# Tokens' operands 64 bytes past multiples of 128 where they stream, at multiples of 128 where weights stream

## The chip, the cores and the metric

The kernel runs on one core of one Trainium2 chip. The metric is the device time of one execution in microseconds (us), the median of several runs. A core has five engines that run side by side: TensorE (PE, matrix products, with its weight loads shown apart as PEld), VectorE (DVE), ScalarE (ACT), GpSimd (POOL) and SyncE (SP), whose queue issues the loads of the weights. Data lie in a memory of 128 partitions; an offset in this text is always in bytes along one partition.

## The reference

What is computed is a stack of transformer-like layers over 256 tokens of width 1024, in float32: a first block of two layers (a recurrent and windowed-attention mixer, a dense feed-forward, a gated delta-rule mixer, a layer of eight experts of which each token uses two), and a second block of two layers, each a feed-forward, a convolution and gating mixer, and a feed-forward.

```python
def swiglu(h, w_gate, w_up, w_down):
    return (jax.nn.silu(h @ w_gate) * (h @ w_up)) @ w_down

# first block, layer 0 and layer 1 (j = 0)
h = h + even_mixer(rms_norm(h, ln_mix[0]), ...)
h = h + swiglu(rms_norm(h, ln_ffn[0]), ...)            # 1024 -> 2816 -> 1024
h = h + gated_deltanet(rms_norm(h, ln_mix[1]), ...)
h = h + moe_swiglu(rms_norm(h, ln_ffn[1]), ...)        # 8 experts, 1024 -> 3584 -> 1024, top 2
# second block, twice
x = x + 0.5 * swiglu_ffn(rms_norm_2(x, ffn1_norm), ...)  # 1024 -> 2816 -> 1024
x = x + mixer(rms_norm_2(x, mix_norm), ...)              # convolution, spatial gate, short convolution
x = x + 0.5 * swiglu_ffn(rms_norm_2(x, ffn2_norm), ...)
```

The result is the last sum after a final norm. All weights, some 590 MB, are read once.

## The kernel before

The residual `X` stays on the chip as [channel, token]: 8 tiles of 128 channels x 256 tokens. Every part reads the norm's operands and adds its product to `X`.

**Single-pass products.** A float32 operand is split into two float32r parts, high and low, and a product is made in three passes: high x high, high x low, low x high. Weights are split by `weights_` (lines 224 to 243): a load of 1 MB into `raw`, then `hi` by ACT (line 231) and `lo` by DVE (line 232), in rings of 4 raw, 5 hi and 5 lo tiles. The tokens' parts are `xh` and `xl`, written by `gain_split` (lines 318 to 324) when a part closes (`acc_close_`, line 308).

**Two ways to multiply.** `mm3` (lines 241 to 250) keeps the weights still, a 128 x 128 block of hi or lo, and streams 256 columns of tokens. `gemm_a` uses it with xh and xl for gates, ups and the mixers' inputs (output tile `bank`); `acc_add` uses it for the products into the residual (output `side`), with the parts `hh` and `hl` of a feed-forward, `yh` and `yl` of the first mixer, or the two halves of `o2` of the delta-rule mixer. `mm3t` (lines 252 to 256) keeps 128 tokens still and streams 512 (in places 256) columns of weights: for q, k and v of the first mixer, the gates of the delta-rule mixer, one product of the later mixers, and all of the experts. A few products of the mixers use whole float32 operands (`mm3` with two operands, line 245) and are not touched.

**Experts.** They run in four pairs. `prep` gathers a pair's tokens, at most 128 for each expert: the even pairs (0 and 2) into tiles of their own, `xeh` and `xel`, the odd pairs (1 and 3) into `xh` and `xl`. An expert takes seven chunks of 512 hidden columns: gate and up are 2 x 8 blocks x 3 passes = 48 matmuls a chunk (336 an expert), the gated product `mh` comes from ACT and DVE (lines 1175, 1176), four transposes, the split into `mhh` and `mhl`, and down, 4 x 2 x 3 = 24 matmuls a chunk (168 an expert). The order of the queues is made by a scheduler from priorities; the change touches none of them.

**Where the operands lie.** Pools are laid one behind the other. The weights' rings start at a multiple of 128 bytes. The tile `p0` has 600 columns, 2400 bytes, which is 96 beyond a multiple of 128, and the tiles behind it inherit that. In the program as built, the bytes beyond a multiple of 128 are:

| tile | before | after | its part in a product |
|---|---|---|---|
| hi, lo | 0 | 0 | still in `mm3`, streams in `mm3t` |
| xh, xl in the mixers and feed-forwards | 96 | 64 | streams in `mm3`; still in the mixers' `mm3t` |
| xh, xl in the experts (odd pairs) | 96 | 0 | still |
| xeh, xel (even pairs) | 0 | 0 | still |
| mhh, mhl | 96 | 0 | still |
| hh, hl of the feed-forwards | 0 | 64 | streams |
| yh, yl of the first mixer | 0 | 64 | streams |
| o2, both halves | 64 | 64 | streams |

The column "after" follows from the diff: 64 for slices that start at element 16 of a tile at a multiple of 128, 0 for `mhh`, whose tiles start at 96 and whose slices start 32 bytes on.

Of the kernel before, what the change touches and what calls it, by code (L numbers as in the profile page):

```python
# [7 lines left out]
F32 = mybir.dt.float32  # L8
F32R = mybir.dt.float32r
I32 = mybir.dt.int32  # L10
AF = mybir.ActivationFunctionType
# [15 lines left out]
W32 = (1, 1, 1, 0)  # L27


# ---------------------------------------------------------------- host layout  # L30
class Pack:
    """Columns of one [128, n] array; name -> column range."""
# [14 lines left out]
def cols(v):  # L47
    """[n*128] -> [128, n], channel c*128+p at [p, c]."""
    return np.asarray(v).reshape(-1, 128).T


def rows(v):
    """[n] on every partition."""
    v = np.asarray(v).reshape(1, -1)
    return np.broadcast_to(v, (128, v.shape[1]))
# [91 lines left out]
# ---------------------------------------------------------------- kernel  # L147
class Builder:
    def __init__(self, ctx, tc, dram, at, out):
# [11 lines left out]
        self.turn, self.half = 0, False  # L161
        self.p0 = self.cp.tile([128, dram["p0"].shape[1]], F32, name="p0")
        self.X = self.cp.tile([128, KD, T], F32, name="X")
        xv = dram["x"].rearrange("(k p) t -> p k t", p=128)
        with tc.high_priority(offset=100000):
            nc.sync.dma_start(self.p0, dram["p0"])
            for k in range(0, KD, 2):
# [6 lines left out]
        self.xh = self.cp.tile([128, KD, T], F32R, name="xh")  # L174
        self.xl = self.cp.tile([128, KD, T], F32R, name="xl")
        # the router takes the gains of its norm
# [3 lines left out]
                                ALU.mult)  # L180

# [10 lines left out]
    def bank(self):  # L192
        """for products with weights"""
        return self.ps.tile([128, 512], F32, name="bank", bufs=4)

    def side(self):
        """for everything else"""
        self.turn = 0 if self.half else 1 - self.turn
        return self.ps.tile([128, 512], F32, name=f"side{self.turn}", bufs=2)

    def other(self):
        """while half is set, what side() leaves"""
        return self.ps.tile([128, 512], F32, name="side1", bufs=2)

    # ---- weights: one raw load, split into two float32r parts
# [7 lines left out]
    def weights(self, ap, kt, n, raw=None, whole=False):  # L213
        """k -> (hi, lo) of rows k*128.. of ap, or those rows themselves"""
# [26 lines left out]
    def mm3(self, out, *ops, start, stop):  # L241
        """three passes over (w hi, w lo, x hi, x lo), or the engine's own float32 product of (w, x)"""
# [15 lines left out]
    # ---- [d, token] products: out rows = columns of W  # L258
    def gemm_a(self, W, c0, n, evac, x32=None):
        """for blocks of up to 512 columns: banks of [128, 2, 256] to evac(bank, first col tile)."""  # L260
# [19 lines left out]
    # ---- products into the residual: 4 banks hold [d, token]  # L280
# [3 lines left out]
    def acc_add(self, W, r0, kt, h, first, last, new=None):  # L284
        """acc += W[r0:r0+kt*128, :]^T h, h whole or in two parts; two k-tiles to a load."""
# [14 lines left out]
    def acc_close(self, scale, gain):  # L300
        """X += scale * acc, with the next norm's operands."""
# [6 lines left out]
    def acc_close_(self, scale, gain):  # L308
        nc = self.nc
        for j in range(4):  # L310
# [15 lines left out]
    # ---- 1/sqrt of small tiles  # L326
# [18 lines left out]
    def rms_(self):  # L345
        """rstd of X over d: [token, 2] and, along the free axis, [128, token]."""
# [45 lines left out]
    # ---- dense feed-forward  # L392
    def ffn(self, wg, wu, wd, nff, scale, gain):
        nc, tc = self.nc, self.tc
        with tc.tile_pool(name="ffn", bufs=2) as pl:
            prev = None
            v2 = lambda t: t.rearrange("p (a t) -> p a t", a=2)
            for f0 in range(0, nff, 512):
                w = min(512, nff - f0)
                hh = pl.tile([128, 4, T], F32R, name="hh")  # L400
                hl = pl.tile([128, 4, T], F32R, name="hl")
# [25 lines left out]
    # ---- recurrent + windowed attention mixer  # L427
    def mixer0(self, gain):
# [3 lines left out]
        with tc.tile_pool(name="mx0", bufs=1) as pl, tc.tile_pool(name="mx0w", bufs=2) as wl:  # L432
            yh = pl.tile([128, 4, T], F32R, name="yh")
            yl = pl.tile([128, 4, T], F32R, name="yl")
            # rope tables with the gains in them
# [9 lines left out]
            # softplus(-lam)  # L445
# [5 lines left out]
            # recurrent input and gates  # L451
# [13 lines left out]
            # q, k, v in [token, column]  # L465
# [28 lines left out]
            # a = exp(-8 r softplus); with t = tanh(4 r softplus) sqrt(1 - a^2) = (1 + a) sqrt(t)  # L494
# [70 lines left out]
            # attention of one block of 128 queries, the even or the odd heads at a time  # L565
# [64 lines left out]
    def softplus(self, pl, out, x, sign, n, tag):  # L630
        """log(1 + exp(sign*x)) = max(sign*x, 0) + 2 atanh(e/(2+e)), e = exp(-|x|)."""
# [18 lines left out]
    # ---- gated delta rule  # L650
    def gdn(self, gain):
# [9 lines left out]
        with tc.tile_pool(name="gd", bufs=1) as pl, tc.tile_pool(name="gdw", bufs=3) as wk, \  # L661
                tc.tile_pool(name="gdd", bufs=1, space=bass.MemoryType.DRAM) as dp:
            # decay and write strength: the last 128 columns of w_in hold them in rows 112..127
# [4 lines left out]
            with first():  # L668
# [23 lines left out]
                # columns: sums around the middle of each block; what follows in block 0  # L692
# [6 lines left out]
                # decays of [j, i]: block 0, block 0 to 1, block 1  # L699
# [18 lines left out]
            # projections with the causal convolution  # L718
# [17 lines left out]
            def sums(src):  # L736
                """|src|^2 + eps of two heads: [token, (m, head)]"""
# [24 lines left out]
            # strictly lower coefficients, transposed: [j, i] of block 0, block 1, block 0 to 1  # L762
# [24 lines left out]
            def evac_q_(bk, c, n):  # L787
                conv(bk, c, qT[:, c:c + 2])
                # eps * 128 * (|q|^2 + eps), what the norm of the unscaled rows adds
# [25 lines left out]
            # y: the coefficients' inverse applied to the values; then outputs [token, d], normed per head  # L815
# [42 lines left out]
            # gates [token, d], then the product as [d, token]  # L858
# [28 lines left out]
    def unit_blocks(self, pl, wk, dp, L):  # L887
        """(I + L)^-1 of the 16 x 16 blocks on the diagonal, one to a partition, and the transposes."""
# [3 lines left out]
        d1 = dp.tile([16, 8, 16, 16], F32, name="d1")         # block and head, b, j, i  # L892
        d2 = dp.tile([2, 16, 8, 16, 16], F32, name="d2")
        lt = pl.tile([128, 272], F32, name="lt")              # [j][i]
        z = pl.tile([128, 272], F32, name="z16")              # [r][c]
# [10 lines left out]
        # 4 x 4 by substitution  # L906
# [9 lines left out]
        # then twice the size: the lower left block is -(right one) (coefficients) (left one)  # L916
# [525 lines left out]
```

## Time and profile before

| | us |
|---|---|
| median of 3 runs | 2518.41 |
| lowest and highest run | 2515.88, 2519.7 |
| span of the profiled execution | 2515.8 |

The stages, by the time at which each closes into the residual: first mixer to 104 us, its feed-forward to 298, delta-rule mixer to 489, experts to 1545, then feed-forward to 1735, mixer to 1835, feed-forward to 2025, feed-forward to 2217, mixer to 2314, feed-forward to the end. The profile counts an engine as busy while an instruction of it is in the works. Matmuls overlap, so a group's mean duration (about 283 ns at 256 columns) is longer than the distance from one start to the next. Where the time order is shown, each row has the start, the duration, the engine, the line and the tiles as out<-in; the stationary and the streamed operand stand behind the arrow.

### The profile page before, as it was taken

How to read it: one execution, taken by the hardware profiler on the slowest of the kernel's cores; microseconds unless marked ns; L12 is line 12 of the kernel's file. 1: busy time of each engine (PE TensorE's matmuls, PEld its weight loads, DVE VectorE, ACT ScalarE, POOL GpSimd, SP SyncE). 2: the span in 40 equal slices, each digit the busy share in tenths (PEclk: the TensorE clock that was granted, in tenths of full speed). 3: DMA queues.
4: the chain of work that ended last, by engine and by line, in shares of the span. 5: the costliest groups of instructions: out<-in, count | busy, mean ns of one | idle time of the engine just before them, and what ended most of it. 6: DMA issues, size and time to landing. Idle time of an engine off the chain costs nothing.

```text
span 2515.8 us, 38995 instructions
## 1 busy us (share of the span) xinstructions
PE 2461.9 (98%) x15762; PEld 2211.6 (88%) x15762; DVE 1885.2 (75%) x2550; ACT 1422.3 (57%) x1761; POOL 19.0 (1%) x41
## 2 busy tenths in 40 slices
PE   7999999999999999999999999999999999999999
PEld 7899999887787778777777778999899999998998
DVE  7765696788988888888898888556865575587554
ACT  6544572477776777777767776445144444443443
POOL 0000000000000000000000000000000000000000
PEclk9999999999999999999999999999999999999999
DMA  6455542589898999999999997554465555545552
GB/s 220 148 176 190 171 140 81 183 293 342 309 334 302 349 343 333 330 351 347 344 324 348 339 353 275 194 170 149 144 207 190 184 168 191 175 131 183 185 184 84
DMA packets 269084, 595.22 MB, mean 237 GB/s; under 512 B 15776, under 2 KB 43808, under 8 KB 268896
## 3 DMA queue, kind: packets, MB, share of 16 engines
q1 hardware_dynamic: 268240, 590.52, 68.3%
q8 instruction: 125, 2.05, 0.3%
q0 software_dynamic: 368, 1.88, 0.2%
q14 instruction: 63, 0.52, 0.1%
q10 hardware_dynamic: 288, 0.26, 0.0%
HBM read 591.18 MB, written 1.44 MB: 236 GB/s over the span
## 4 chain that ended last, share of the span: by engine, by line
PE 57%; DVE 8%; ACT 2%; DMA 2%; issue 1%; DVEq 0%; ACTq 0%
PE bank L249 7%; PE bank L250 7%; PE bank L248 7%; PE bank L255 6%; PE bank L256 6%; PE bank L254 6%; PE side L249 3%; PE side L248 3%; PE side L250 3%; DVE av L1287 3%; DVE lo L232 3%; PE side L254 2%; PE side L255 2%; PE side L256 2%; ACT hi L231 2%
## 5 line engine op out<-in xcount | busy, mean ns | idle before, releaser
L232 DVE TENSOR_TENSOR lo<-raw,hi 128x1024 fp32r<-128x1024 f32 (+1 forms) x1077 | 1270.4, 1217 | 397.8 <-ACT hi L231 390.6
L231 ACT CAST hi<-raw 128x1024 fp32r<-128x1024 f32 (+1 forms) x1077 | 1081.0, 1046 | 573.4 <-PE bank L249 249.9
L248 PE MATMUL bank<-xh,hi 128*128 128x256 f32 x2152 | 608.6, 283 | 15.4 <-ACT hi L231 11.0
L249 PE MATMUL bank<-xl,hi 128*128 128x256 f32 x2152 | 610.9, 284 | 0.3
L250 PE MATMUL bank<-xh,lo 128*128 128x256 f32 x2152 | 609.5, 284 | 0.0
L248 PEld LDWEIGHTS bank<-xh,hi 128*128 128x128 f32 x2152 | 408.8, 190 | 17.0 <-ACT hi L231 11.0
L249 PEld LDWEIGHTS bank<-xl,hi 128*128 128x128 f32 x2152 | 406.5, 189 | 1.2 <-DVE xl L323 0.9
L250 PEld LDWEIGHTS bank<-xh,lo 128*128 128x128 f32 x2152 | 405.8, 189 | 0.3
L249 PE MATMUL side<-hl,hi 128*128 128x256 f32 x880 | 249.2, 283 | 0.0
L250 PE MATMUL side<-hh,lo 128*128 128x256 f32 x880 | 249.1, 283 | 0.0
L248 PE MATMUL side<-hh,hi 128*128 128x256 f32 x880 | 249.0, 283 | 0.0
L255 PE MATMUL bank<-lo,xh 128*128 128x512 f32 (+1 forms) x544 | 215.2, 396 | 6.3 <-DVE lo L232 6.3
L254 PE MATMUL bank<-hi,xh 128*128 128x512 f32 (+1 forms) x544 | 211.3, 388 | 4.0 <-PEq L1074 4.0
L256 PE MATMUL bank<-hi,xl 128*128 128x512 f32 (+1 forms) x544 | 210.7, 387 | 0.0
L255 PE MATMUL bank<-lo,xeh 128*128 128x512 f32 x448 | 178.1, 397 | 4.7 <-DVE lo L232 4.2
L255 PE MATMUL side<-lo,mhh 128*128 128x512 f32 x448 | 181.4, 405 | 0.5 <-DVE lo L232 0.2
L254 PE MATMUL bank<-hi,xeh 128*128 128x512 f32 x448 | 175.8, 392 | 1.1 <-ACT hi L231 1.1
L256 PE MATMUL side<-hi,mhl 128*128 128x512 f32 x448 | 176.9, 397 | 0.0
L256 PE MATMUL bank<-hi,xel 128*128 128x512 f32 x448 | 175.1, 391 | 0.0
L250 PEld LDWEIGHTS side<-hh,lo 128*128 128x128 f32 x880 | 168.9, 192 | 0.0
L248 PEld LDWEIGHTS side<-hh,hi 128*128 128x128 f32 x880 | 168.8, 192 | 0.0
L249 PEld LDWEIGHTS side<-hl,hi 128*128 128x128 f32 x880 | 168.8, 192 | 0.0
(421 smaller groups left out, 2894.1 us busy)
## 6 DMA issues: line engine op xcount, KB each, us to landing
raw<-in_o_moe_w_down_dram SPq DMA_DIRECT2D x112, 1024.0 KB, 6.8
raw<-in_o_moe_w_up_dram SPq DMA_DIRECT2D x111, 1024.0 KB, 7.0
raw<-in_o_moe_w_gate_dram SPq DMA_DIRECT2D x109, 1024.0 KB, 7.0
raw<-in_ffn_w_gate_dram SPq DMA_DIRECT2D x44, 1024.0 KB, 5.2
raw<-in_ffn_w_up_dram SPq DMA_DIRECT2D x44, 1024.0 KB, 5.1
raw<-in_ffn_w_down_dram SPq DMA_DIRECT2D x44, 1024.0 KB, 5.1
raw<-in_o_w_in_dram SPq DMA_DIRECT2D x16, 1024.0 KB, 5.4
raw<-in_w_in_dram SPq DMA_DIRECT2D x20, 768.0 KB, 4.5
```

Of the source, the lines that this page charges most:

```text
L231: nc.scalar.copy(hi[:, :w], src)
L232: nc.vector.tensor_tensor(lo[:, :w], src, hi[:, :w], ALU.subtract)
L248: nc.tensor.matmul(out, wh, xh, start=start, stop=False, skip_group_check=True)
L249: nc.tensor.matmul(out, wh, xl, start=False, stop=False, skip_group_check=True)
L250: nc.tensor.matmul(out, wl, xh, start=False, stop=stop, skip_group_check=True)
L254: nc.tensor.matmul(out, xh, wh, start=start, stop=False, skip_group_check=True)
L255: nc.tensor.matmul(out, xh, wl, start=False, stop=False, skip_group_check=True)
L256: nc.tensor.matmul(out, xl, wh, start=False, stop=stop, skip_group_check=True)
L1287: nc.vector.scalar_tensor_tensor(av[:, c], ca[:, c, j:j + T], caw[:, c, j:j + 1], av[:, c], ALU.mult, ALU.add)
```

## The change

The tiles of xh and xl grow by 32 columns, are made first in their pool (so they start at a multiple of 128), and `place` sets which slice of them is in use: element 0 for the step "ffn1", the experts, and element 16 (64 bytes) for every other step. `acc_close_` calls it before it writes the next step's operands. hh, hl, yh and yl come from `stream`, a tile with 32 columns more of which the slice from element 16 is used. mhh and mhl get 32 columns more and a slice from element 8, 32 bytes on, which puts them at multiples of 128. Nothing else of the program differs, apart from comments.

```diff
+OFF = 16
@@ Builder.__init__
+        self.xs = [self.cp.tile([128, KD * T + 32], F32R, name=n) for n in ("xh", "xl")]
+        self.place("mix0")
         self.p0 = self.cp.tile([128, dram["p0"].shape[1]], F32, name="p0")
...
-        self.xh = self.cp.tile([128, KD, T], F32R, name="xh")
-        self.xl = self.cp.tile([128, KD, T], F32R, name="xl")
...
+    def place(self, step):
+        o = 0 if step == "ffn1" else OFF
+        self.xh, self.xl = (t[:, o:o + KD * T].rearrange("p (k t) -> p k t", k=KD) for t in self.xs)
+
+    def stream(self, pool, k, name):
+        t = pool.tile([128, k * T + 32], F32R, name=name)
+        return t[:, OFF:OFF + k * T].rearrange("p (k t) -> p k t", k=k)
@@ acc_close_
         nc = self.nc
+        if gain is not None:
+            self.place(gain)
@@ ffn
-                hh = pl.tile([128, 4, T], F32R, name="hh")
-                hl = pl.tile([128, 4, T], F32R, name="hl")
+                hh, hl = self.stream(pl, 4, "hh"), self.stream(pl, 4, "hl")
@@ mixer0
-            yh = pl.tile([128, 4, T], F32R, name="yh")
-            yl = pl.tile([128, 4, T], F32R, name="yl")
+            yh, yl = self.stream(pl, 4, "yh"), self.stream(pl, 4, "yl")
@@ moe_pass
-                hh, hl = wk.tile([128, 4, 128], F32R, name="mhh"), wk.tile([128, 4, 128], F32R, name="mhl")
+                hh, hl = (wk.tile([128, 544], F32R, name=n)[:, 8:520].rearrange("p (a t) -> p a t", a=4)
+                          for n in ("mhh", "mhl"))
```

## Rows read from the trace of the kernel before

**Rows 1.** The page's head: span, and busy time and share of each engine.

```profile
span 2515.8 us, 38995 instructions
PE 2461.9 (98%) x15762; PEld 2211.6 (88%) x15762; DVE 1885.2 (75%) x2550; ACT 1422.3 (57%) x1761; POOL 19.0 (1%) x41
```

**Rows 2.** Stages: length, busy us by engine, PE clock, DMA share, GB/s.

```profile
107.00:310.00 203.00, 202.83 (x1683) 201.94 (x1683) 128.02 (x164) 95.72 (x113) 3.98 (x5) 1.00 0.55 183
310.00:500.00 190.00, 183.58 (x1386) 171.92 (x1384) 148.26 (x365) 94.77 (x172) 4.34 (x5) 0.99 0.40 129
1020.00:1280.00 260.00, 255.47 (x1151) 203.84 (x1150) 224.95 (x219) 187.63 (x209) 0.00 (x0) 1.00 0.97 343
1740.00:1810.00 70.00, 68.07 (x413) 61.62 (x413) 64.82 (x164) 16.86 (x29) 0.00 (x0) 1.00 0.45 143
```

**Rows 3.** The chain of work, 1740 to 1810 us, shares by line.

```profile
by line: DVE av L1287 53.4%; DVE lo L232 9.3%; issue 5.1%; DVE t L1235 3.7%; DVE cc L1306 3.4%; PE side L245 1.9%; ACT hi L231 1.5%; DVE cb L1235 1.3%; DVE cc L1235 1.3%; DVE y L1314 1.3%; PE bank L250 1.2%; PE bank L248 1.2%; PE bank L249 
```

**Rows 4.** PE in time order, 256 columns: start us, us, line, tiles, count.

```profile
199.92 0.28 PE L249 MATMUL bank<-xl,hi 128*128 128x256 f32 x1
...
206.04 0.28 PE L249 MATMUL bank<-xl,hi 128*128 128x256 f32 x1
...
221.88 0.28 PE L249 MATMUL side<-hl,hi 128*128 128x256 f32 x1
...
228.00 0.28 PE L249 MATMUL side<-hl,hi 128*128 128x256 f32 x1
...
463.05 0.28 PE L249 MATMUL side<-o,hi 128*128 128x256 f32 x1
...
465.99 0.28 PE L250 MATMUL side<-o,lo 128*128 128x256 f32 x1
...
469.38 0.28 PE L249 MATMUL side<-o,hi 128*128 128x256 f32 x1
...
480.94 0.28 PE L249 MATMUL side<-o,hi 128*128 128x256 f32 x1
```

**Rows 5.** PE in time order, experts, 512 columns, weights streaming.

```profile
1096.12 0.39 PE L255 MATMUL bank<-lo,xeh 128*128 128x512 f32 x1
...
1101.11 0.39 PE L256 MATMUL bank<-hi,xel 128*128 128x512 f32 x1
...
1300.26 0.40 PE L254 MATMUL bank<-hi,xh 128*128 128x512 f32 x1
...
1305.89 0.40 PE L254 MATMUL bank<-hi,xh 128*128 128x512 f32 x1
...
1309.37 0.40 PE L255 MATMUL side<-lo,mhh 128*128 128x512 f32 x1
...
1311.47 0.40 PE L256 MATMUL side<-hi,mhl 128*128 128x512 f32 x1
```

**Rows 6.** Groups by line, whole span: count, busy us, mean ns, idle.

```profile
L248 PE MATMUL bank<-xh,hi 128*128 128x256 f32 x2152 | 608.6, 283 | 15.4 <-ACT hi L231 11.0 <-ACT xh L322 2.2 <-ACT lg L491 2.1
...
L248 PE MATMUL side<-hh,hi 128*128 128x256 f32 x880 | 249.0, 283 | 0.0
```

**Rows 7.** DVE in time order: line 1176 in experts 4 and 6.

```profile
1039.43 0.74 DVE L1176 SCALAR_TENSOR_TENSOR mh<-bank,gs,mh 128x512 f32<-128x512 f32 x1
...
1140.89 0.75 DVE L1176 SCALAR_TENSOR_TENSOR mh<-bank,gs,mh 128x512 f32<-128x512 f32 x1
...
1297.33 0.74 DVE L1176 SCALAR_TENSOR_TENSOR mh<-bank,gs,mh 128x512 f32<-128x512 f32 x1
...
1399.83 0.74 DVE L1176 SCALAR_TENSOR_TENSOR mh<-bank,gs,mh 128x512 f32<-128x512 f32 x1
```

**Rows 8.** Stages, two stretches of experts 4 and 6.

```profile
1039.40:1140.90 101.50, 99.73 (x435) 78.29 (x434) 86.42 (x82) 72.77 (x80) 0.00 (x0) 1.00 0.98 353
1297.30:1399.80 102.50, 100.90 (x435) 78.53 (x434) 86.56 (x81) 72.33 (x79) 0.00 (x0) 1.00 0.98 348
```

**Rows 9.** Load queue waits, 500 to 1545 us: total us, times, longest.

```profile
SPq L209 <- DVE lo L232: 889.4, 329, 12.3
```

## The prediction

> **What bounds the kernel now.** I read the page's head first: PE is busy 98% of a span of 2515.8 us, DVE 75%, ACT 57% [rows 1]. An average hides stages, so the second view is the busy time by stage [rows 2]. In the first dense feed-forward (107 to 310 us) PE works 202.83 of 203 us, while DVE stands at 128 and the DMA engines near half: PE alone sets the time there, and the four later ones are the same code. In the delta-rule mixer (310 to 500) PE has 183.58 of 190. In the first of the two later mixers (1740 to 1810) PE is busy 68.07 of 70 and DVE 64.82, and the chain of work decides: 53.4% of it is DVE's long convolution [rows 3]. In the experts (1020 to 1280) PE is busy 255.47 of 260, but the DMA engines are at 0.97 as well, so two resources are near their end together.
>
> A busy PE says nothing of its pace, because matmuls overlap in the trace. The pace is the distance from one start to the next. The change alters nothing but where operands begin, and the kernel before already holds several cases of this, side by side, so the trace can price it. Which tile lies where is in the table ahead of this.
>
> 256 columns, weights stationary at 0: tokens streamed from 96 (xh, xl) take 51 steps in 199.92 to 206.04, 120.0 ns each; tokens streamed from 0 (hh, hl) take 51 steps in 221.88 to 228.00, 120.0 ns; tokens streamed from 64 (the parts of o2, product of the delta-rule mixer) take 102 steps in 469.38 to 480.94, 113.3 ns [rows 4]. Same lines, same shape, and in all three the chip granted PE its upper clock level of 2.4 GHz (1.00, or 0.99 over the stage, in [rows 2]). One exception has to be kept: o2's first k-tile, 463.05 to 465.99, runs 25 steps at 117.6 ns at the same offset.
>
> 512 columns, weights streaming from 0: tokens stationary at 0 (xeh, xel) take 22 steps in 1096.12 to 1101.11, 226.8 ns; at 96 (xh, xl used for odd pairs) 24 steps in 1300.26 to 1305.89, 234.6 ns; at 96 (mhh, mhl) 9 steps in 1309.37 to 1311.47, 233.3 ns [rows 5].
>
> **Part by part.** No instruction is added, removed or moved, and no DMA. Moving xh by 64 bytes makes a k-slice overlap two old slices, so a write of xh could wait for readers of both; all those readers are products that PE finishes before the products into the residual, whose last one the write waits for anyway. Nothing is queued behind a new wait. The extra bytes in SBUF cost no time.
>
> *Dense feed-forward, five times.* Gate and up are 2 x 22 x 8 = 352 blocks, down 176, three passes each: 528 x 3 = 1584 matmuls, 7920 in all; of the 2152 rows a pass for xh [rows 6] these are 1760, and all 880 of hh. Both streams go to 64. The saving is 120.0 - 113.3 = 6.7 ns each: 7920 x 6.7 = 53.1 us. Nothing hides it, since PE has no idle time in the stage, and what is late next is far off: at 113.3 ns a feed-forward needs 1584 x 0.1133 = 179 us where DVE works 128 and DMA about 0.55 x 203 = 112 us [rows 2]. The low end of the gain is o2's first k-tile: 120.0 - 117.6 = 2.4 ns, 19 us. I take 113.3, since seven of o2's eight k-tiles run so, through stalls and transposes in between.
>
> *Delta-rule mixer and small mixers.* The same offset for 2152 - 1760 = 392 blocks of xh and mixer0's 32 of yh, three passes: 1272 x 6.7 = 8.5 us. The later mixers hold 384 of these matmuls; part stands beside the convolution on DVE [rows 3], so I count half of their 2.6 us, and of the other 5.9 all but 0.7, for stretches that wait on DVE's chains: 6.5 us, ends 3 and 8.5. Here tokens also stand still at 64 while weights stream (q, k, v, the delta-rule gates, the values of the later mixers): 144 matmuls of 512 columns and 144 of 256. No row has that combination. Its neighbours are 226.8 ns at 0 and 234.6 at 96, so 7.8 ns either way, 288 x 7.8 = 2.2 us gain or loss; I take 0, no change from today, which lies between these ends.
>
> *Experts.* Gate and up of the odd pairs go from 96 to 0: 4 experts x 336 = 1344 matmuls x (234.6 - 226.8) = 10.5 us. Down of all experts too: 8 x 168 = 1344 x (233.3 - 226.8) = 8.7 us. Together 19.2 us of PE time. How much of it arrives is read from two like stretches, from an expert's first product of gate and up on DVE (mh, line 1176) to its seventh. Expert 4 has its tokens at 0, expert 6 at 96, otherwise the same work: 288 gate and up matmuls, so 288 x 7.8 = 2.2 us apart in pace. They take 101.5 us (1039.43 to 1140.89) and 102.5 (1297.33 to 1399.83), 1.0 apart [rows 7]. So 0.45 of the pace arrived. The reason stands beside it: DMA at 0.98 in both stretches, 353 and 348 GB/s [rows 8]. The queue of loads waits 889.4 us for raw buffers that DVE frees [rows 9], so a faster PE does ask for loads sooner, but the engines have 2% left. I take 19.2 x 0.45 = 8.7 us, ends 0 and 19.2. The Trainium skill ("HBM Reference", Specifications) says that a core streaming alone gets about 425 GB/s; by it the experts, at about 350, would have room, the whole 19.2 would arrive and the sum would be 10.5 us better. The 0.98 of the rows speaks against it, and they decide.
>
> Sum: 53.1 + 6.5 + 8.7 = 68.3 us. The profiled execution's span is 2515.8 us, against a median of 2518.41 of the runs, which reach from 2515.88 to 2519.7; the 2.6 us between lie around the span or in the runs' own spread, and the change touches neither. 2518.4 - 68.3 = 2450.1 us.
>
> **Rivals.**
> *Two paces at 64.* Whether a stream at 64 settles at 113.3 or 117.6 ns may depend on how it was entered, and long unbroken feed-forward streams keep what they start with. If half of them hold 117.6, the feed-forwards give 0.5 x 53.1 + 0.5 x 19 = 36 us, the mixers 4, the experts 8.7: 49 us, 2469.6 us. All of them at 117.6, 19 + 2 + 8.7: 2489 us. For: 25 steps in [rows 4]. Against: the next k-tile is entered by the same four transposes and does settle.
> *The offset is not the cause.* o2's product could be faster for another reason, as its stage. Then only the experts' gain stands, and with DMA at its end perhaps not even that: 2510 to 2518 us. A page has this as a rule: the Trainium skill ("TensorE: Matmul & The Clock Gate", Wait — 56ns, not 53.3ns?) gives the distance of warm matmuls as columns over 2.4 GHz plus 2.5 ns, with no word of addresses; by it 256 columns take 109 ns wherever they lie, and the time stays at 2518. The trace disagrees: 113.3 and 120.0 ns for the same shape, both above 109. Against the rival as such: xeh and xh differ by 7.8 ns in the same code of the same stage [rows 5].
> *Slower: the two parts collide.* The parts now lie 8320 bytes apart (xh, xl) and 4224 (hh, hl) instead of 8192 and 4096. If the second pass starting in the other half of a 256-byte line costs what an unlucky start costs now, 6.7 ns more than today instead of less, on every pass, 9192 x 6.7 = 62 us come on top, less 8.7: about 2571 us. It decides from the point at which more than half of the passes pay, as then the mean exceeds 120.0. Against it: parts 8192 and 4096 apart both run at 120.0 [rows 4]; no row has an odd multiple of 128.
> *Experts fully bound by DMA*: 2518.4 - 59.6 = 2458.8 us; *not bound*: 2439.6 us. Both lie within the forecast's own range.
>
> **How the numbers follow.** Forecast with its experts' ends 0.85; two paces 0.08; offset not the cause 0.04; slower 0.03. The time is the forecast's, 2450. The forecast alone reaches from 2518.4 - 53.1 - 8.5 - 2.2 - 19.2 = 2435 to 2518.4 - 53.1 - 3 + 2.2 - 0 = 2464.5. The range takes in also the half-way case of two paces: 2435 to 2472. About 0.2% (5 us) is what a measurement can tell from no change. Faster by more: forecast, two paces and a part of the third, 0.94; within 0.2%: 0.03; slower 0.03.
>
> **What would show it.** In the profile after, xh, xl, hh and hl steps of 113.3 ns in every feed-forward, so that a stage of 190 us loses 10 to 11; expert 6's stretch at about 101 us with DMA at 0.98 or more, gate and up at 226.8 ns and down too; mixers nearly as long as before. Steps of 117.6 ns in whole feed-forwards would bear out the first rival, 120.0 the second, and steps of hi with xl alone above 120 the third. If the experts lose 19 us, DMA was not at its end and my factor of 0.45 is wrong.

## The result, and the profile after

The changed kernel takes 2488.28 us (median of 4 runs, 2487.47 to 2490.13) against 2517.93 us before: a ratio of 0.9883, 95% interval 0.9871 to 0.9895. The forecast was 2450 us with a range from 2435 to 2472. The sign is right, the gain is 30 us instead of 68, and the time lies outside the range.

The head of the page after: span, then busy time, share and count of each engine. It answers [rows 1].

```profile
span 2485.8 us, 38995 instructions
PE 2430.1 (98%) x15762; PEld 2187.8 (88%) x15762; DVE 1884.9 (76%) x2550; ACT 1422.0 (57%) x1761; POOL 19.9 (1%) x41
```

Same counts, nearly the same shares: PE's own time fell by 31.8 us, the span by 30.0. PE is still what the kernel waits for. Busy time by stage after (stretch, length, busy us and count of PE, PEld, DVE, ACT and POOL, PE clock, DMA share, GB/s), a feed-forward and the experts, answers [rows 2]:

```profile
107.00:295.00 188.00, 187.58 (x1597) 186.98 (x1596) 118.00 (x139) 88.35 (x103) 3.61 (x2) 1.00 0.57 188
1020.00:1280.00 260.00, 255.28 (x1160) 204.92 (x1159) 225.77 (x220) 187.77 (x208) 0.00 (x0) 1.00 0.97 344
```

Nothing new ends last: PE fills the feed-forward at the upper clock level (1.00, 2.4 GHz), and the experts still have PE and DMA near their ends. So the question is PE's pace. PE in time order after, 256 columns (start us, us, line, tiles, count), first and last row of four unbroken stretches: the high and low parts of xh, hh in its first buffer, hh in its second, and o2.

```profile
204.81 0.28 PE L259 MATMUL bank<-xh,hi 128*128 128x256 f32 x1
...
217.68 0.28 PE L261 MATMUL bank<-xh,lo 128*128 128x256 f32 x1
...
218.15 0.28 PE L259 MATMUL side<-hh,hi 128*128 128x256 f32 x1
...
225.93 0.28 PE L259 MATMUL side<-hh,hi 128*128 128x256 f32 x1
...
252.07 0.28 PE L259 MATMUL side<-hh,hi 128*128 128x256 f32 x1
...
259.91 0.28 PE L259 MATMUL side<-hh,hi 128*128 128x256 f32 x1
...
466.74 0.28 PE L259 MATMUL side<-o,hi 128*128 128x256 f32 x1
...
478.40 0.28 PE L259 MATMUL side<-o,hi 128*128 128x256 f32 x1
```

110 steps of xh at 117.0 ns, 66 of hh at 117.9, 69 of hh in its other buffer at 113.6, and 99 of o2 at 117.8. Two things stand out. The two buffers of hh, written and read by the same lines, differ by 4.3 ns. And o2, whose offset the change left alone, slowed from the 113.3 ns of [rows 4] to 117.8.

Offsets beyond a multiple of 128, as the prediction counted them, can't tell the buffers of hh apart: both are 64. Taken beyond a multiple of 256 they can. In the program as built, hi and lo lie at 128 beyond a multiple of 256, before and after. Below, the distance of an operand is its own place minus that of the weights, within 256 bytes (so +64 and -64 differ, and -128 is the farthest).

| operand | distance before | distance after | mean step before | after |
|---|---|---|---|---|
| xh, xl (streams) | +96, +96 | +64, -64 | 120.0 ns | 117.4 ns |
| hh, hl, first buffer | 0, 0 | +64, +64 | 119.9 | 117.8 |
| hh, hl, second buffer | 0, 0 | -64, -64 | 119.9 | 114.3 |
| o2, both halves | -64 | -64 | 114.1 | 117.5 |
| xh, xl still, experts | +96, +96 | 0, -128 | 234.2 | 231.4 |
| mhh still, one buffer pair | +96 | -128 | 234.2 | 232.7 |
| mhh still, the other pair | +96 | 0 | 234.2 | 227.9 |

The means are over all undisturbed steps of the span, with each matmul of the trace joined to its operands' addresses in the program. A tile of 8320 bytes is an odd multiple of 128, so xl lands on the other side of the weights than xh; tiles of 4224 bytes do the same to successive buffers. The experts in time order after, 512 columns, odd pair, answer [rows 5]:

```profile
1291.65 0.40 PE L266 MATMUL bank<-lo,xh 128*128 128x512 f32 x1
...
1296.73 0.40 PE L267 MATMUL bank<-hi,xl 128*128 128x512 f32 x1
```

22 steps at 230.9 ns, between the 234.6 and 226.8 of [rows 5].

By stage (from one stage's last addition to X to the next one's) the five feed-forwards went from 966.3 to 944.6 us, the experts from 1055.5 to 1048.9, and the mixers from 494.0 to 492.3: 21.7, 6.6 and 1.6 us before rounding, which is the whole difference of the spans, 30.0 us.

### The profile page after: what moved, and what is told of

The parts are those of the page before. It is cut to its first block, busy times and chain, and to the rows that moved or that the text cites. A ratio compares the mean times of both kernels' runs of the same rounds, so it can differ in the third digit from the quotient of the medians.

```text
span 2485.8 us, 38995 instructions
## 1 busy us (share of the span) xinstructions
PE 2430.1 (98%) x15762; PEld 2187.8 (88%) x15762; DVE 1884.9 (76%) x2550; ACT 1422.0 (57%) x1761; POOL 19.9 (1%) x41
## 4 chain that ended last, share of the span: by engine, by line
PE 56%; DVE 8%; ACT 2%; issue 1%; DMA 1%; DVEq 0%; ACTq 0%
PE bank L266 7%; PE bank L261 6%; PE bank L260 6%; PE bank L259 6%; PE bank L267 6%; PE bank L265 6%; PE side L260 3%; PE side L261 3%; PE side L259 3%; DVE av L1299 3%; DVE lo L243 3%; PE side L265 3%; PE side L266 2%; PE side L267 2%; ACT hi L242 2%
```

## The experiments

Theory A: what counts is the distance between the two operands within 256 bytes, and both token parts have to lie alike; the change misses 113.3 ns because its parts don't. Rivals: the absolute place counts; the pace depends on how the stream was entered; the DMA engines eat the experts' gain. In the table "us" is the median of a kernel's runs, while the stage lengths (us) come from the one execution that was traced; for e5 that is the quickest of its four, for e4 the slowest.

| kernel | distance of the streams | us | ratio to before (95%) | feed-forwards | experts |
|---|---|---|---|---|---|
| before | +96; 0 | 2517.9 | | 193.9 189.7 190.8 191.4 200.6 | 1055.5 |
| the change | +64/-64; +64 or -64 | 2488.3 | 0.9883 (0.9871 to 0.9895) | 189.7 185.4 186.4 187.0 196.0 | 1048.9 |
| e1 | -64 | 2454.8 | 0.9760 (0.9743 to 0.9776) | 184.3 180.2 180.0 182.0 190.9 | 1043.6 |
| e2 | +64 | 2475.7 | 0.9824 (0.9806 to 0.9842) | 190.8 186.4 186.4 181.9 190.9 | 1043.9 |
| e3 | many | 2493.5 | one run | 191.2 186.0 186.6 190.2 199.5 | 1046.8 |
| e4 | as the change | 2492.9 | 0.9901 (0.9885 to 0.9918) | 189.7 185.4 186.4 187.3 196.3 | 1055.4 |
| e5 | -64, weights moved | 2475.9 | 0.9842 (0.9823 to 0.9861) | 184.4 180.2 181.0 188.3 191.0 | 1048.4 |
| e6 | -64 high, +64 low | 2489.9 | 0.9890 (0.9873 to 0.9906) | 190.8 186.4 186.4 188.3 197.4 | 1043.4 |
| e7 | -64 | 2493.4 | one run | 190.8 186.4 187.4 181.9 197.3 | 1056.1 |
| e8 | -64 | 2447.0 | one run | 184.4 192.5 186.4 188.3 197.3 | 1004.1 |
| e9 | +64, with entries | 2503.0 | one run | 193.0 188.2 188.7 190.5 199.6 | 1045.0 |
| e10 | -64, with entries | 2468.9 | one run | 186.8 182.2 183.2 184.4 193.3 | 1043.7 |
| e11 | -64, with entries | 2483.7 | one run | 186.8 182.2 183.5 184.4 193.7 | 1056.8 |

**Both parts on one side.** e1 puts every streamed part 64 bytes short of the weights and every still part of the experts on the weights' own class; the tiles grow by 64 columns, so successive tiles stay alike.

```diff
-OFF = 16
+OFF = 48
...
-        self.xs = [self.cp.tile([128, KD * T + 32], F32R, name=n) for n in ("xh", "xl")]
+        self.xs = [self.cp.tile([128, KD * T + 64], F32R, name=n) for n in ("xh", "xl")]
...
-        t = pool.tile([128, k * T + 32], F32R, name=name)
+        t = pool.tile([128, k * T + 64], F32R, name=name)
...
-                hh, hl = (wk.tile([128, 544], F32R, name=n)[:, 8:520].rearrange("p (a t) -> p a t", a=4)
+                hh, hl = (wk.tile([128, 576], F32R, name=n)[:, 40:552].rearrange("p (a t) -> p a t", a=4)
```

> The tiles grow by 64 columns instead of 32, so both parts and both buffers lie alike modulo 256: every streamed token operand 64 bytes below the weights' class (192 above it modulo 256), every stationary one of the experts in the weights' class. Theory A (the place modulo 256 relative to the weights sets the pace): all streams at 113.3 to 114.5 ns. From 117.4 for xh that is 6456 x 3.5 = 23 us, from 117.8 for the first buffer of hh 1440 x 4 = 6 us, the experts' gate and up of odd pairs and half of down 3 to 4 ns faster each, some 5 us of which arrive; about 34 us less than the changed kernel, 2454 us. Theory B (only modulo 128 counts, and whether a stream settles at 113.3 or 117.6 is decided by how it was entered): the mixture stays, 2485 to 2491 us.

Measured 2454.8 us (2453.8, 2455.7, 2461.8, 2453.9). PE in time order of e1, in a late feed-forward and in an odd pair of the experts:

```profile
1899.93 0.28 PE L259 MATMUL bank<-xh,hi 128*128 128x256 f32 x1
...
1909.90 0.28 PE L260 MATMUL side<-hl,hi 128*128 128x256 f32 x1
...
1282.83 0.39 PE L266 MATMUL bank<-lo,xh 128*128 128x512 f32 x1
...
1285.77 0.39 PE L267 MATMUL bank<-hi,xl 128*128 128x512 f32 x1
```

88 steps at 113.3 ns, across both kinds of product, and 13 at 226.2 in the experts. The feed-forwards gain 48.9 us on before, the experts 11.9, the mixers 3.3: together 64, near the 68.3 of the prediction's sum. This is the version that beats both kernels.

**The other side.** e2 is e1 with `OFF = 16`: both parts 64 bytes past the weights.

> As the run before, but the streams lie 64 bytes above the weights' class modulo 256 instead of 64 below; the same place modulo 128. Theory A: all streams of xh and hh at 117.8 ns and none at 113.3, the experts as in the run before: 6456 x 0.4 + 1200 x 3.4 = 6.5 us more and some 5 us less than the changed kernel, about 2490 us. Theory B: hh and xh keep stretches at 113.3 ns, as today about 0.4 of hh; 2480 to 2488 us.

Measured 2475.7 us (2475.2, 2476.1, 2467.8, 2476.1). PE in time order of e2, in two neighbouring feed-forwards:

```profile
1899.89 0.28 PE L261 MATMUL side<-hh,lo 128*128 128x256 f32 x1
...
1909.90 0.28 PE L259 MATMUL bank<-xh,hi 128*128 128x256 f32 x1
...
2079.91 0.28 PE L261 MATMUL bank<-xh,lo 128*128 128x256 f32 x1
...
2090.00 0.28 PE L260 MATMUL side<-hl,hi 128*128 128x256 f32 x1
```

85 steps at 117.8 ns and 89 at 113.4: the same code at the same distance. DVE in time order of e2, the last addition to X of three stages, shows that it holds for the whole stage:

```profile
1815.91 0.69 DVE L325 SCALAR_TENSOR_TENSOR X<-side,X 128x512 f32<-128x512 f32 x1
...
2002.32 0.69 DVE L325 SCALAR_TENSOR_TENSOR X<-side,X 128x512 f32<-128x512 f32 x1
...
2184.21 0.68 DVE L325 SCALAR_TENSOR_TENSOR X<-side,X 128x512 f32<-128x512 f32 x1
```

186.4 us and then 181.9, where e1 takes 180.0 and 182.0 for the same two stages. About 1500 matmuls keep one of two paces without a change between them; in the traces of e1, e2, e5 and e7 to e11, whose streamed parts lie alike, none of the 319 unbroken stretches of 27 steps and more (every step within 112 to 120 ns, the longest 1570 steps) mixes the two. The time is below what either theory expected, and theory A alone is not enough: there are two paces at +64, as the prediction's first rival said of 64. The third run, 7.8 us below the others, fits one more feed-forward at the quicker pace, but it has no trace here.

**Other distances.** e3 is e1 with an offset of its own for each step.

```diff
+XOFF = {"ffn1": 0, "ffn0": 32, "f1_0": 40, "f2_0": 56, "f1_1": 44, "f2_1": 52}
+HOFF = {"ffn0": 8, "f1_0": 4, "f2_0": 60, "f1_1": 36, "f2_1": 47}
...
-        o = 0 if step == "ffn1" else OFF
+        self.step = step
+        o = XOFF.get(step, OFF)
...
+        o = HOFF.get(self.step, OFF)
```

> One look at many offsets. Parts and buffers alike modulo 256; bytes above the weights' class modulo 256, for xh and xl in the five feed-forwards in order: 128, 160, 224, 176, 208; for hh and hl: 32, 16, 240, 144, 188; elsewhere 192. Theory A: each offset has a pace of its own, near 120 ns between 0 and 32 and at 224 to 240, 117 to 120 at 128, and from 144 to 208 a fall towards 113.3. Theory B: offsets of the same place modulo 128 are alike, so xh at 128 runs as 0 does (120.0), hh at 188 as 64 (113.3 or 117.6), and nothing depends on 128 against 0. The time is some 2465 to 2485 us in both.

Measured 2493.5 us, above the 2465 to 2485 that was expected. Mean steps at each distance, parts alike, all undisturbed triples (the three passes over one block; 0 and +96 from before, +64 from e2):

| distance | -128 | -112 | -96 | -80 | -68 | -64 | -48 | -32 | -16 | 0 | +16 | +32 | +64 | +96 |
|---|---|---|---|---|---|---|---|---|---|---|---|---|---|---|
| ns | 118.7 | 118.7 | 118.0 | 119.3 | 119.3 | 114.8 | 119.2 | 118.3 | 117.2 | 119.9 | 116.7 | 117.0 | 116.0 | 120.0 |

Four bytes decide: -68 takes 119.3 ns, -64 in the same run (its mixers) 114.8. No distance tried is below 113.3 in any stretch, and 113.3 is kept over whole stages only 64 bytes to either side. Neither theory's list came out: there is no gradual fall towards -64, and places alike beyond 128 are not alike (-128 takes 118.7 ns, 0 takes 119.9). Most of the distances were tried in one feed-forward of this one run, so a second pace at one of them is not excluded.

**The streams alone.** e4 is the change without the experts' part: there xh and xl stay at +96 and -32, mhh and mhl as they were.

```diff
-        o = 0 if step == "ffn1" else OFF
+        o = 24 if step == "ffn1" else OFF
...
-                hh, hl = (wk.tile([128, 544], F32R, name=n)[:, 8:520].rearrange("p (a t) -> p a t", a=4)
-                          for n in ("mhh", "mhl"))
+                hh, hl = wk.tile([128, 4, 128], F32R, name="mhh"), wk.tile([128, 4, 128], F32R, name="mhl")
```

> The change without its part for the experts: there xh, xl, mhh and mhl lie 96 beyond a multiple of 128 as before; the streams are as in the change. By the two traces the experts gained 6.6 us and the feed-forwards 21.9. If these are separate, this kernel is at 2488 + 6 = 2494 to 2495 us with gate and up of odd pairs and down at 234 ns. If the experts are held by DMA and their gain was chance, 2488 to 2490.

Measured 2492.9 us, with the experts at 1055.4 us as before the change and the feed-forwards as after it. The two parts of the change are separate, and the experts' part is worth 6.5 us of stage time, or 4.6 us between the medians.

**Relative or absolute.** e5 is e1 with small tiles ahead of the weights' rings and behind them: the weights move by 64 bytes, and with `OFF = 0` the tokens' streams lie where hh and hl lay in the kernel before.

```diff
-OFF = 48
+OFF = 0
...
+        self.sp1 = pool("sp1", 1)
         self.hip = pool("hip", 5)
...
+        self.sp2 = pool("sp2", 1)
         self.cp = pool("cp", 1)
...
+        for p, n in ((self.sp1, 16), (self.sp2, 48)):
+            nc.gpsimd.memset(p.tile([128, n], F32, name=f"gap{n}"), 0.0)
```

> The rings of hi and lo are pushed 64 bytes up by a gap in front of them, and a second gap puts everything behind back; tokens lie at multiples of 128 where they stream, as hh did in the kernel before, parts alike modulo 256. So the distance of tokens to weights is what it was in e1, minus 64, but no streamed operand lies 64 past a multiple of 128. If the distance counts: streams hold 113.3 or 117.8 ns for whole feed-forwards and never 120.0, some 180 to 187 us each; with the experts' tokens now 64 away from the weights that stream, their pace is unknown, 227 to 235 ns, so 2455 to 2485 us. If the absolute place counts: 120.0 ns, feed-forwards of 190 us, 2505 us or more.

Measured 2475.9 us (2465.9, 2479.0, 2483.3, 2472.7). PE in time order of e5, in the first feed-forward and in a late one:

```profile
214.86 0.28 PE L264 MATMUL side<-hl,hi 128*128 128x256 f32 x1
...
222.79 0.28 PE L265 MATMUL side<-hh,lo 128*128 128x256 f32 x1
...
2049.92 0.28 PE L265 MATMUL bank<-xh,lo 128*128 128x256 f32 x1
...
2059.93 0.28 PE L263 MATMUL bank<-xh,hi 128*128 128x256 f32 x1
```

113.3 ns (70 steps) and 117.8 (85 steps), where the same places of the tokens gave 120.0 before. The distance counts, not the place. And -64 can have the slower pace too, which fits o2 after the change. The four runs of this one kernel lie 17.4 us apart, more than two feed-forwards' change of pace (6.3 us for the fourth, 188.3 against e1's 182.0); that the pace differs from run to run is the likely reason, but one run alone has a trace.

**Parts unlike.** e6 is e1 with the low parts alone 128 bytes off.

```diff
+        l = o if step == "ffn1" else o - 32
-        self.xh, self.xl = (t[:, o:o + KD * T].rearrange("p (k t) -> p k t", k=KD) for t in self.xs)
+        self.xh, self.xl = (t[:, o_:o_ + KD * T].rearrange("p (k t) -> p k t", k=KD) for t, o_ in zip(self.xs, (o, l)))
...
+        o = OFF - 32 if name[1] == "l" else OFF
-        return t[:, OFF:OFF + k * T].rearrange("p (k t) -> p k t", k=k)
+        return t[:, o:o + k * T].rearrange("p (k t) -> p k t", k=k)
```

> As e1, but the low parts of streamed tokens (xl, hl, yl) lie 128 bytes below the high parts modulo 256, so one part is 64 below the weights' class and the other 64 above; both still 64 past a multiple of 128. If unlike parts are what kept the change from 113.3: no long stretch at 113.3 in any feed-forward, a mean of about 117.5 ns for xh and for hh, 9192 x 3.9 = 35 us above e1, 2490 us. If each feed-forward simply settles at one of two paces by how it is entered: whole feed-forwards at 113.3 remain, 2455 to 2480 us.

Measured 2489.9 us, 35 above e1. PE in time order of e6:

```profile
2049.85 0.28 PE L261 MATMUL side<-hh,hi 128*128 128x256 f32 x1
...
2059.98 0.28 PE L263 MATMUL side<-hh,lo 128*128 128x256 f32 x1
```

117.8 ns (86 steps), and not one stretch of the five feed-forwards at 113.3. That could also be the slower of the two paces, met five times. Against it: no undisturbed triple of the streams in e6 (2971 of them) and none of xh in the change (2059) has a mean step below 115.0 ns, while in e7 and e8 below, with parts alike and four feed-forwards of five at the slower pace, 26% of the triples of xh and hh are below 114.5. The steps differ as well: 115 to 122 ns within e6's row, 117 to 119 within e2's slower one. With parts unlike, the quick pace was never entered: the trap of the change's xh and xl.

**Still tokens at other places.** e7 is e1 with another offset for each pair's tokens and each expert's mhh and mhl.

```diff
+PAIR = (16, 48, 8, 40)
+DOWN = (40, 56, 8, 24, 48, 44, 32, 36)
...
```

> One look at many offsets of the experts' tokens, which stand still; streams as in e1. Bytes above the weights' class modulo 256: xeh or xh of the four pairs 64, 192, 32, 160; mhh and mhl of the eight experts 0, 64, 128, 192, 32, 16, 224, 240. If the distance modulo 256 sets this pace too: 226.7 to 228 ns at 0, 229 to 233 at 64 and 192 (the first mixer's tokens stood at those), 231 at 128, 234 at 32, 160, 224 and other places off multiples of 64. If only modulo 128 counts: 0 and 128 alike, 64 and 192 alike. Time between e1 and 2470 us.

Measured 2493.4 us, above the 2470 that was expected at most. Steps of 512 columns by the distance of the still tokens, all kernels together: 0: 227.7 ns; -16: 228.1; -64: 229.1; +64: 233.3; -128: 232.7; +16: 232.3; -96, -32 and +32: 233.2; +96: 234.2. Here 0 is best, while for streams it is among the worst. The experts took 1056.1 us instead of 1043.6. The streams are e1's, yet four feed-forwards of five slowed to 117.8 ns. PE in time order of e7, in one of them:

```profile
1899.84 0.28 PE L263 MATMUL bank<-xh,lo 128*128 128x256 f32 x1
...
1909.97 0.28 PE L262 MATMUL side<-hl,hi 128*128 128x256 f32 x1
```

These are 86 steps of 117.8 ns. Whether the edit in another stage moved the pace, or this one execution got it by chance, as e5's runs suggest, is not shown.

**Is DMA at its end in the experts?** e8 is e1 without the low-weights pass (`lo` with the high token part) in gate, up and down of the experts, a third of their PE work.

```diff
-        nc.tensor.matmul(out, xh, wl, start=False, stop=False, skip_group_check=True)
+        if lo:
+            nc.tensor.matmul(out, xh, wl, start=False, stop=False, skip_group_check=True)
...
```

> Leaves out the experts' second pass (tokens high times weights low), so their output is not the reference's; loads, splits and everything else as in e1. It asks how far the DMA engines are from their end in the experts. PE work falls by about 300 us there. If DMA ends at what 0.98 of its time gave, some 353 to 360 GB/s: 352 MB take 978 to 997 us, the experts go from 1043 to about 1000 and the kernel from 2455 to some 2410, DMA share at 0.99. If it has room to 400 GB/s and more, the next bound is DVE with some 16.1 us for each of 56 chunks: the experts at about 920 to 960 us, the kernel at 2340 to 2370.

The experts took 1004.1 us, 39.5 less than in e1. The whole kernel took 2447.0 us and not the expected 2410, mostly because four feed-forwards of five, which this edit doesn't touch either, ran at the slower pace: the five took 948.9 us, where e1 has 917.4. Two views of e8, 1020 to 1480 us, all within the experts: the busy time of PE, PEld, DVE, ACT and POOL as above, and the DMA engines (total and mean; the load queue's packets, MB and share):

```profile
1020.00:1480.00 460.00, 348.68 (x1463) 240.47 (x1462) 410.32 (x396) 346.85 (x382) 0.00 (x0) 1.00 1.00 359
DMA packets 69180, 165.07 MB, mean 359 GB/s; under 512 B 2519, under 2 KB 2519, under 8 KB 69158
q1 hardware_dynamic: 69158, 164.80, 99.3%
```

The DMA view of e1, 1010 to 1517 us:

```profile
DMA packets 73970, 175.70 MB, mean 347 GB/s; under 512 B 2680, under 2 KB 2680, under 8 KB 73940
q1 hardware_dynamic: 73940, 175.31, 97.2%
```

With a third of PE's work gone the rate rises from 347 to 359 GB/s and no further, with the load queue at 99.3% of the engines' time and DVE, the next, busy 410 of 460 us: the loads set a floor near 1004 us, which the experts of e1 exceed by 4%.

**Where the pace is chosen.** e9 and e10 are e2 and e1 with a small product ahead of each block of 512 columns in `gemm_a`, ten in a feed-forward, so that TensorE leaves its row of products and enters it again.

```diff
             banks = [self.bank() for _ in range((nb + 1) // 2)]
+            if w == 512:
+                self.nc.tensor.matmul(banks[0][:, 0:128], self.ones, self.ident, start=True, stop=True)
```

> The streams as in e2_stream_plus64 (both parts 64 bytes past the weights' class), with one small float32 product (128 columns, into a bank that the next block opens anew) put ahead of each 512-column block of the streamed side, so that TensorE leaves and re-enters its row of single-pass products about ten times in each feed-forward. The product is only an interruption; nothing reads it. Theory, the pace is set at an entry and then kept: inside one feed-forward stretches at 113.3 ns and at 117.8 ns now stand beside one another, and each change of pace falls on one of the small products or on another interruption, none between them; some of the feed-forwards that ran whole at 117.8 in e2 become mixed. Rival, the pace follows from the place of the operands alone: each block keeps the pace that it had in e2. The time is 2475 plus some 50 products at 0.3 to 0.4 us, 2490 to 2495, less up to 7 us for each feed-forward that turns to 113.3.

> The same small products in e1_stream_minus64 (both parts 64 bytes short of the weights' class), whose feed-forwards all ran at 113.3 ns. Theory, the pace is set at an entry: with some fifty more entries several stretches fall to 117.8 ns, and the time rises by more than the products themselves cost: 2454 plus 15 to 20 us for the products, 2470 to 2474, plus up to 35 us if all turn. Rival, at 64 bytes short the pace is 113.3 by the place alone: no stretch at 117.8, 2470 to 2474.

e9: 2503.0 us. Behind each of 49 small products of the feed-forwards (the scheduler drew the fiftieth forward, into the experts) the pace was 117.8 ns, also in the two stages that ran at 113.3 in e2; neither expectation fits, since the first wanted a mixture and the second the paces of e2. PE in time order of e9, 83 steps behind one of them:

```profile
1847.04 0.28 PE L259 MATMUL bank<-xh,hi 128*128 128x256 f32 x1
...
1856.82 0.28 PE L261 MATMUL bank<-xh,lo 128*128 128x256 f32 x1
```

e10: 2468.9 us, with 113.3 ns behind 47 of the 49. PE in time order of e10 around one of the other two (L277 is the small product):

```profile
1819.82 0.39 PE L277 MATMUL bank<-p,ones 128*128 128x128 f32 x2
...
1820.16 0.28 PE L260 MATMUL bank<-xl,hi 128*128 128x256 f32 x1
...
1831.12 0.28 PE L260 MATMUL bank<-xl,hi 128*128 128x256 f32 x1
1831.23 0.28 PE L261 MATMUL bank<-xh,lo 128*128 128x256 f32 x1
1831.35 0.38 PE L277 MATMUL bank<-p,ones 128*128 128x128 f32 x2
...
1832.83 0.28 PE L261 MATMUL bank<-xh,lo 128*128 128x256 f32 x1
...
1841.90 0.28 PE L260 MATMUL bank<-xl,hi 128*128 128x256 f32 x1
```

1820.16 to 1831.12 are 93 steps of 117.8 ns, and behind the next small product 80 steps of 113.4. The pace changes at the interruption, and not between two.

**The same entries where the slower pace ruled.** e11 puts e10's products into e7.

> The small float32 products of e9 and e10 in e7_still_offsets, whose streams lie as in e1_stream_minus64 (both parts 64 bytes short of the weights' class) but whose feed-forwards ran whole at 117.8 ns in four cases of five. In e10 all but one of some fifty blocks behind such a product ran at 113.3, in e9 all at 117.8. Theory, an entry behind this product settles the pace by the side on which the streams lie: from the first product of each feed-forward on, all blocks run at 113.3, the feed-forwards take what they took in e10 (186.8, 182.2, 183.2, 184.4 and 193.3 us where e7 had 190.8, 186.4, 187.4, 181.9 and 197.3), and the whole about 2493 minus 14 for these plus 2 for the products elsewhere, 2478 to 2484. Rival, the pace belongs to the stage or the run and the product only interrupts: stretches at 117.8 remain through four feed-forwards, and the products add their 2.3 us to each, 2504 to 2510.

Measured 2483.7 us, 9.7 less than e7 in spite of its added products. The feed-forwards take 186.8, 182.2, 183.5, 184.4 and 193.7 us, e10's lengths within 0.4 us. PE in time order of e11, in the stage that ran at 117.8 ns in e7:

```profile
1847.71 0.28 PE L262 MATMUL bank<-xl,hi 128*128 128x256 f32 x1
...
1855.98 0.28 PE L263 MATMUL bank<-xh,lo 128*128 128x256 f32 x1
```

73 steps at 113.3 ns. The word "all" of the expectation was too strong: 45 of the 49 products led to 113.3, four to 117.8. e7 and e11 are one run each, so the difference between their stages could again be the execution's. Within one stage it can't: in e10 and e11 blocks at 117.8 ns are followed, behind the next small product, by blocks at 113.3 of the same code, so the stage doesn't own the pace.

## Why the prediction was wrong, step by step

**What bounds the kernel.** Right. PE fills the feed-forwards (187.58 of 188 us), nothing was added, and every microsecond gained is a change of pace.

**Feed-forwards, 53.1 us: this step failed.** It took 113.3 ns as the pace of any stream 64 bytes off. Measured 21.7. By the means of the first table: xh 5280 x 2.6 = 13.7 us, hh in its first buffer (12 of 22 k-tiles) 1440 x 2.1 = 3.0, in its second 1200 x 5.6 = 6.7, together 23.4. Two facts were missed. Offsets were counted beyond multiples of 128, though no row could show that this is enough: o2, the only stream at 64, lay on one side of the weights with both its parts alike, and those of xh would not. e1 and e6 differ in the low parts' side alone and are 35 us apart. And one exception in [rows 4], 25 steps at 117.6 ns, was the second of two paces, which can last a whole stage. With parts alike at -64 the step was worth 48.9 us in e1's trace: direction and size held for a condition that the change doesn't meet. Even that condition doesn't ensure it: in the traces of e1, e5, e7 and e8, all alike at -64, five, four, one and one of the five feed-forwards ran at 113.3 ns. So alike parts were needed (e6) but not enough, and e1's 48.9 us are the best case.

**Mixers, 6.5 us.** Measured 1.6, for the same reason; o2 lost its quick pace besides, 192 matmuls x 3.4 ns = 0.7 us. With 3.3 in e1 the term was too large even there. Still tokens at +64 and -64 took 231.8 ns where the trace before has 234.2, inside the bounds given.

**Experts, 8.7 us.** Measured 6.6, from two errors that offset each other. The saving of PE time was not 19.2 us: xl and one pair of mhh lie 128 bytes off the weights' class, so it was 1344 x 2.8 for gate and up and 1344 x 3.9 for down, 9.0 us. And 6.6 of 9.0 arrived, 0.73 and not 0.45; in e1 it is 11.9 of 1344 x (6.2 + 6.5) = 17.1 us, 0.70. The 0.45 came from one pair of stretches [rows 7], 1.0 us against 2.2, too small a difference to carry a factor. That DMA is near its end was right (e8). The Trainium skill ("HBM Reference", Specifications) gives about 425 GB/s for a core streaming alone; with PE's work cut by a third the experts reached 359 (e8), so the trace doesn't bear that figure out for these loads.

**The rivals.** "Two paces at 64", all at the slower one, gave 2489 us, the measured time; the match is partly luck, as the streams' means were 117.4, 117.8 and 114.3 ns and not one pace. Half of its mechanism is shown: e2 has both paces in one kernel at one distance. But in the change xh's parts are unlike and none of its triples had the quick pace, with no choice at an entry (e6). "The two parts collide" named that very place, the odd multiple of 128, and priced it with the wrong sign: 117.4 ns, not 126.7. As two of the rivals touch what no row had shown (whether a stream keeps 113.3 ns, and what an unlike pair does), 0.85 for the forecast was too much, and a range ending at the half-way case too narrow. "The offset is not the cause" fell: in e5 the streams lie where hh lay before, the weights 64 bytes further, and the steps take 113.3 or 117.8 ns instead of 120.0.

**Still open.** Why an entry leads to one pace or the other, and how much of it the program decides and how much the execution. Shown is that the pace holds from one interruption to the next, that behind the small float32 product it was 113.3 ns 92 times of 98 at -64 (e10, e11) and 117.8 all 49 times at +64 (e9), and that other entries go either way (e2, e5, e7). What inside TensorE or the memory does this, no run shows.

## What to carry to other kernels

When a pace seems to follow from an operand's place, price it by its distance to the other operand, test every part of the product for it, and look at where padding puts the next buffer. Where equal instructions show two paces in one trace, expect that the whole stream may get the rarer one, and judge a change by several runs and not by one. And take a factor for "how much arrives" from a difference that is large against the spread of the stretches it is read from.

## What the runs showed of the hardware

- Single-pass products of 256 columns ran at 113.3 to 120.0 ns a step at one granted clock (1.00), by the distance between streamed and still operand within 256 bytes; at 512 columns, with the weights streaming, from 226.2 to 234.6.
- For a stream 64 bytes to either side there are two paces, 113.3 and 117.8 ns, each held for up to some 1500 matmuls (e2). A kernel's runs differ by steps of 7 to 8 us, about what one feed-forward's change of pace is worth (e1 2453.8 and 2461.8, e2 2475.2 and 2467.8); that this is the reason is not traced.
- One small float32 product ahead of a block, some 0.2 us each (e10's feed-forwards are 2.0 to 3.2 us longer than e1's, for ten), can bring the quicker pace back at -64 (e10, e11).
